# Hyena gates as seven-product pairs in the attention stage; values and token sums in the hyena stage

## The chip, the cores and the metric

The kernel runs on one core of a Trainium2 chip. The core has TensorE (PE; its weight loads are listed as PEld), VectorE (DVE), ScalarE (ACT), GpSimd (POOL) and SyncE (SP), and 16 DMA engines. DMAs are issued from the queues of SP, ACT and POOL. The metric is the time of one execution in device microseconds. The median of three runs of the kernel before is 900.05 us (899.94 to 900.84).

## The reference

One layer works on 128 context tokens and 512 latent tokens, 640 in all, with 1024 channels. After an adaLN modulation, `h = x * (1 + scale) + shift`, one projection `z = h @ w_in` gives twelve groups of 1024 columns: three for the hyena branch, its gate, queries, keys, values, the attention gate, and two merge gates.

- Hyena branch: a three-tap convolution over the three groups, `u = v_h * x1`, a long convolution of `u` with filters made by a small network (by Fourier transform), then `y_h = (conv + u * d) * x0`.
- Attention branch: 16 heads of 64. The latent tokens attend to a clamped window with a learned two-dimensional bias and to 128 cached context keys, in one softmax; the context tokens attend to themselves.
- Merge: `p_h = (y_h * silu(g_h)) @ w_bh`, `p_a = (y_a * silu(g_a)) @ w_ba`, `out = (sigmoid(m_h) * p_h + sigmoid(m_a) * p_a) @ w_out`, then `layer_norm(alpha * x + gate * out)`.

The context tokens' keys and values are outputs too.

## The kernel before, in words

Channels lie on the 128 partitions, tokens along the free dimension: a row is 128 x 640. The modulated input stays on chip as two parts, `hH` (rounded to the matmul's format) and `hL` (the rest), and so does every weight: high x high, low x high and high x low are the three passes of each product. A weight tile covers 128 output channels and all 1024 input channels; its high part is an ACT copy and its low part a difference.

There are two ways to project. `proj` does one tile: 8 blocks of input channels x 3 passes x 2 halves of 320 columns = 48 matmuls. `pair_tile` does two tiles at once by a seven-product scheme: it needs sums and differences of four weight quarters (`wsum`, 128 x 512, line 1027, in the pool `sp`), their high and low parts (`prep`, which calls `split`, lines 101 and 102), token sums `t1` to `t4` of `hH` and `hL` (`token_sums`), and 7 x 4 x 3 = 84 matmuls of 320 columns (line 1054), then a few additions of results (lines 1061 to 1069). Weight parts go round in a ring of five buffers.

The stages follow one another. The *prologue* makes the modulation. The *hyena stage* runs four quarters of two row tiles. For each, `quarter_head` projects and convolves the values and x1, and `quarter_tail` projects x0 and the gate; both use `proj` with the low part of the weights completed by an accumulating DMA on POOL's queue (`wtile` with "dma", lines 147 to 149). The long convolution (`long_conv`, `long_conv_back`) and the next filter (`filter_spectrum`) are woven into these projections by `weave`, which steps two generators in a given ratio. `gated` products of rows (`gapped_product`, lines 457 and 461) are DVE work; a finished row goes to DRAM as `yh_d`. The fourth tail is the *hand-over* (`hand_over`), which is woven with the last convolution and also does queries, keys and values 0, attention gate 0, and queries, keys and values 1. When the convolution is done, `attention_setup` closes its buffer pools and opens those of attention (`sp`, `tp`, `at`).

The *attention stage* goes through eight pairs of heads (`attend`), each woven with other projections (`mains`). In heads 0 and 1 these are three `proj` tiles each and the token sums, on DVE; from head 2 on, pairs (`queries_keys`, `gates_a`, `mix` for the merge gates), two values and one single gate. The softmax's bias comes from a mask and a table, subtracted on POOL for each head (`bias_tile`, lines 807 to 811), and POOL normalizes the probabilities (lines 840 and 891). The *merge* projects both branches, and the output with its norm comes last.

A planner decides the order on each engine from the program's order and its own estimate of times. PE's order is the program's own in the prologue and in attention; loads of the prologue keep their order, too. A buffer's tag with `bufs` slots makes the next user wait for a free slot.

## Time and profile before

| | us |
|---|---|
| median of three runs | 900.05 |
| span of the profiled execution | 898.9 |
| PE busy | 878.5 |
| DVE busy | 625.1 |
| ACT busy | 423.6 |
| POOL busy | 161.6 |

The profile is of one execution; its span runs from the first to the last instruction. Stages are read by stretches of the span: the hyena loop lies between 57 and about 285 us, the hand-over reaches to about 385, attention runs to 715, the merge and output to the end. In tables of stages, each engine has its busy time and, in brackets, its number of instructions in that stretch. In lists of groups, the part behind the first bar is busy time, the mean duration of one in ns, then the idle time of the engine just before them and what ended it. In a tile's or a line's list, durations are shortest/median/longest in ns. In an engine's order of time, the first number is the start, the second the duration, `x` the number of instructions merged in the row.

### The profile page before, as it was taken

Reading aid. Unit: us, or ns where it says so; the run is one execution under the profiler, and the core shown is the slowest. Engines: PE = TensorE matmul, PEld = TensorE weight load, DVE = VectorE, ACT = ScalarE, POOL = GpSimd, SP = SyncE. Lnnn points to the kernel's source line nnn. Section 1 sums busy time; section 2 is a strip of 40 time slices with the busy share of each in tenths; the row PEclk is TensorE's granted clock in tenths of the full one; section 3 lists DMA queues with packets and bytes.
Section 4 is the critical chain, followed back from the end, with each engine's and each line's share of the span. In section 5 each row is a group of like instructions: output and inputs, shape, how many; then the busy total and the mean of one; then the engine's idle time right before and its main releaser. Section 6 shows DMA issues by size and latency. Waiting matters only on the chain. (4 is left out here: it accounts for less than half of the span.)

```text
span 898.9 us, 16950 instructions
## 1 busy us (share of the span) xinstructions
PE 878.5 (98%) x6560; PEld 848.8 (94%) x6560; DVE 625.1 (70%) x1229; ACT 423.6 (47%) x909; POOL 161.6 (18%) x188
## 2 busy tenths in 40 slices
PE   8999999999999999999999999999999999999994
PEld 7899999999999999999999999899999999999883
DVE  4776784794778568578877578766766668667665
ACT  4495455645445342365566455555655522233100
POOL 0010010101001000086654321332332000000000
PEclk9999999999999999999999999999999999999997
DMA  9975665665647223333233332332343588355332
GB/s 335 384 170 130 136 136 118 152 129 125 157 101 153 62 69 90 93 106 92 57 126 116 104 97 90 118 117 92 102 135 106 171 298 286 133 178 172 114 103 85
DMA packets 56715, 124.43 MB, mean 138 GB/s; under 512 B 8603, under 2 KB 28059, under 8 KB 56636
## 3 DMA queue, kind: packets, MB, share of 16 engines
q1 hardware_dynamic: 46988, 103.07, 35.6%
q0 software_dynamic: 4032, 14.68, 10.1%
q10 hardware_dynamic: 5616, 5.61, 1.8%
q8 instruction: 52, 0.85, 0.4%
q14 instruction: 27, 0.22, 0.1%
HBM read 109.18 MB, written 14.16 MB: 137 GB/s over the span
## 5 line engine op out<-in xcount | busy, mean ns | idle before, releaser
L168 PE MATMUL mm<-hH,wh 128*128 128x320 f32 x672 | 160.2, 312 | 1.8 <-ACT zs L471 1.0
L168 PE MATMUL mm<-hH,wl 128*128 128x320 f32 x672 | 158.5, 310 | 0.5 <-DVE wl L102 0.4
L168 PE MATMUL mm<-hL,wh 128*128 128x320 f32 x672 | 158.6, 311 | 0.0
L168 PEld LDWEIGHTS mm<-hH,wh 128*128 128x128 f32 x672 | 112.9, 188 | 4.7 <-issue 1.8
L168 PEld LDWEIGHTS mm<-hH,wl 128*128 128x128 f32 x672 | 113.5, 188 | 1.5 <-DVE wl L102 0.9
L168 PEld LDWEIGHTS mm<-hL,wh 128*128 128x128 f32 x672 | 113.3, 188 | 1.1 <-DVE hL L315 0.5
L1054 PE MATMUL sp<-t,wb 128*128 128x320 f32 x672 | 105.4, 310 | 0.0
L1054 PEld LDWEIGHTS sp<-t,wb 128*128 128x128 f32 x672 | 99.5, 188 | 0.3 <-issue 0.3
L1054 PE MATMUL sp<-hH,wb 128*128 128x320 f32 x336 | 82.1, 313 | 0.6 <-DVE c L1069 0.5
L101 ACT ACTIVATE wh<-raw 128x1024 fp32r<-128x1024 f32 x37 | 39.1, 1060 | 71.4 <-PE mm L168 41.5
L148 POOL DMA_DIRECT2D wl<-wall x28 | 24.4, 871 | 261.8 <-ACT wl L147 224.2
L102 DVE TENSOR_TENSOR wl<-raw,wh 128x1024 fp32r<-128x1024 f32 x37 | 45.8, 1240 | 26.4 <-ACT wh L101 26.2
L1054 PEld LDWEIGHTS sp<-hH,wb 128*128 128x128 f32 x336 | 57.9, 188 | 2.8 <-issue 1.7
L149 ACT ACTIVATE wh<-raw 128x1024 fp32r<-128x1024 f32 x28 | 29.7, 1060 | 52.7 <-PE mm L168 52.6
L101 ACT ACTIVATE wb<-s 128x512 fp32r<-128x512 f32 x56 | 34.7, 626 | 40.8 <-DVE s L1027 27.7
L102 DVE TENSOR_TENSOR wb<-s,wb 128x512 fp32r<-128x512 f32 x56 | 39.0, 702 | 19.4 <-ACT wb L101 19.1
L1054 PE MATMUL sp<-hL,wb 128*128 128x320 f32 x168 | 51.8, 309 | 0.0
L840 POOL TENSOR_SCALAR p<-p,sm 128x384 f32<-128x384 f32 x32 | 45.2, 1422 | 25.7 <-DVE sm L839 25.7
L1288 PE MATMUL out<-woh,yhs 128*128 128x512 f32 (+1 forms) x176 | 45.5, 372 | 0.0
L168 PE MATMUL mm<-yhs,wh 128*128 128x320 f32 x224 | 42.6, 309 | 0.0
L840 POOL TENSOR_SCALAR edge<-edge,sm 128x320 f32<-128x320 f32 x32 | 42.1, 1326 | 2.8 <-DVE sm L839 2.8
L1288 PEld LDWEIGHTS out<-woh,yhs 128*128 128x128 f32 x176 | 32.0, 188 | 6.0
(358 smaller groups left out, 2028.9 us busy)
## 6 DMA issues: line engine op xcount, KB each, us to landing
raw<-wall SPq DMA_DIRECT2D x96, 512.0 KB, 3.7
wl<-wall POOLq DMA_DIRECT2D x28, 512.0 KB, 5.6
ada<-wada SPq DMA_DIRECT2D x16, 512.0 KB, 8.2
gate<-wgate SPq DMA_DIRECT2D x8, 512.0 KB, 4.3
wo<-wall SPq DMA_DIRECT2D x8, 512.0 KB, 4.3
xt<-xT SPq DMA_DIRECT2D x8, 320.0 KB, 7.9
dec<-decay SPq DMA_DIRECT2D x20, 128.0 KB, 3.2
yh_d<-yh SPq DMA_DIRECT2D x8, 320.0 KB, 2.5
```

What stands on the lines that cost most here:

```text
L101: hi = nc.scalar.activation(dst_h, src, AF.Copy)
L102: return hi, (eng or nc.vector).tensor_tensor(dst_l, src, f(dst_h), op=ALU.subtract)
L148: nc.gpsimd.dma_start(wl, a["wall"][i], accum_op=ALU.add)
L149: nc.scalar.activation(wh, raw[:], AF.Copy)
L168: nc.tensor.matmul(ps[hf][:, :HALF], wt[k], x[:, hf * HALF : (hf + 1) * HALF], start=(i == 0 and k == 0), stop=(i == lead[2] and k == NK - ...
L840: nc.gpsimd.tensor_scalar_mul(pv, pv, sm[:, 2:3])
L1054: nc.tensor.matmul(dst, wk, x(xi, k), start=j < 4 and k == 0 and i == 0, stop=k == 3 and i == 2, skip_group_check=True,)
L1288: ins = nc.tensor.matmul(dst, m[k][:, c0 : c0 + P], w[:, c : c + n], start=(first and k == 0), stop=(last and k == 5), skip_group_check=True,)
```

## The change

- The eight hyena gates leave the hyena stage. `quarter_tail` keeps only x0, now in the pool `yhp`. Its product with the convolution's result is made on POOL (`product_in_blocks`) and goes to DRAM as `yu_d`. In attention four pairs (`gates_h`) make the gates, POOL multiplies each half row by the reloaded product, and the result goes to `yh_d` from POOL's queue.
- All attention gates are pairs (a0, a2, a4, a6), and so are queries and keys 2 and 3. Heads have their pairs from a list, 22 in all.
- Values 1, 2 and 3 are projected in the three quarters of the hyena loop, go to DRAM (`v_d`) and are loaded again before heads 2, 4 and 6. Values 0 stay in the hand-over.
- The token sums are made on POOL during the hyena loop, a piece at every sixth step, stored to DRAM (`tok_d`) from POOL's queue and loaded in `attention_setup`.
- A pair's weights are prepared by a generator of their own (`prepared`), one product ahead at each product done, the ring of five running on from pair to pair. One of the four weight sums and three of the seven low parts are on POOL.
- The bias of each head comes ready from the host, 128 x 1024, with signs of scores turned; mask and table are gone.

```diff
+    def product_in_blocks(y, x, u):
+        nc.gpsimd.tensor_tensor(y[:, :LP], x[:, :LP], u[:, :LP], op=ALU.mult)
+        (xs, us), yb = (by_row(t[:, GAP:NG]) for t in (x, u)), y[:, SC : SC + LS]
+        for b0, n, bs in ((0, 1, slice(7, 8)), (1, 7, slice(0, 7))):
+            nc.gpsimd.tensor_tensor(from_blocks(yb[:, 64 * b0 : 64 * (b0 + n)], n), xs[:, :, bs], us[:, :, bs], op=ALU.mult)
...
     def gate_conv(n):
         if n in half_done:
-            gapped_product(out["yh"][n], out[f"u{n // 2}"][n % 2])
-            nc.sync.dma_start(yh_d[n], out["yh"][n][:])
+            y = row(yhp, "yh", f"yu{n}")
+            product_in_blocks(y, out["x0"].pop(n), out[f"u{n // 2}"][n % 2])
+            nc.gpsimd.dma_start(yu_d[n], y)
...
-            x0 = hwa.tile([P, NG + 1], F32, tag="cv", bufs=2, name=f"x0_{n}")
-            yield from conv_tile(16 + n, x0)
-            yield
-            yh[n] = row(yhp, "yh", f"yh{n}")
-            yield from gate_tile(24 + n, yh[n][:], "dma")
-            gapped_product(yh[n], x0)
+            out["x0"][n] = row(yhp, "yh", f"x0_{n}", n=NG + 1)
+            yield from conv_tile(16 + n, out["x0"][n])
             gate_conv(n)
...
     for q in range(3):
-        weave(chain(quarter_head(q + 1), quarter_tail(q)), chain(long_conv(q), braid(long_conv_back(q), filter_spectrum(q + 1))),
-              8 * NK, N_CONV + N_BACK + N_FILTER)
+        weave(along(chain(quarter_head(q + 1), quarter_tail(q), values((2, 3, 1)[q], v_d)), sums, 6),
+              chain(long_conv(q), braid(long_conv_back(q), filter_spectrum(q + 1))), 6 * NK + N_VALUES, N_CONV + N_BACK + N_FILTER)
...
-        yield from chain(queries(0), keys(0), values(0), gate_a(0), queries(1))
+        yield from chain(queries(0), keys(0), values(0), queries(1))
         out["slots_r"] = left.enter_context(tc.tile_pool(name="slots_r", bufs=1))
-        yield from chain(keys(1), values(1))
+        reload_values(1)
+        yield from keys(1)
...
+    ON_POOL = dict(sums=(3,), lows=(0, 4, 5))
...
+        for j in range(7):
+            if j == 3:
+                wsum(3, a21, a22, ALU.add)
+                wsum(6, a12, src[1], ALU.add, src[1])
+            n = len(made)
+            w = made[i0, j] = wp.tile([P, 2, 512], F32R, tag=RING[n % 5], bufs=2 if RING[n % 5] == "wh" else 3, name=f"wb{i0}_{j}")
+            split(w[:, 0], w[:, 1], src[j], nc.gpsimd if j in ON_POOL["lows"] else None)
+            yield
...
+    def gates_h(m):
+        yu = {}
+        for i, hf in ((1, 1), (0, 0), (1, 0), (0, 1)):
+            yu[i, hf] = halfrow("yu", 3, f"yur{m}{i}{hf}")
+            load_to(yu[i, hf], yu_d[2 * m + i][:, CS[hf]])
+
+        def use(i, hf, src):
+            th = halfrow("th", 2, f"th{m}{i}{hf}")
+            nc.scalar.activation(th, src, AF.Tanh, scale=0.5)
+            gate(th, src)
+            nc.gpsimd.tensor_tensor(th, th, yu[i, hf], op=ALU.mult)
+            nc.gpsimd.dma_start(yh_d[2 * m + i][:, CS[hf]], th)
...
-    weave(hand_over(), chain(long_conv(3), long_conv_back(3), attention_setup()), 6 * NK + N_VALUES, N_CONV + N_BACK + 1)
+    weave(hand_over(), chain(long_conv(3), long_conv_back(3), attention_setup()), 4 * NK + N_VALUES, N_CONV + N_BACK + 1)
...
+    HEADS = ("a0 h0", "q2 h1 m0", "q3 m1 a2", "q4 h2 m2", "q5 m3 a4", "q6 h3 m4", "q7 m5 a6", "m6 m7")
```

The new `token_sums` does the same additions as before on `nc.gpsimd`, and for each sum makes the two parts there and stores both:

```diff
+        def keep(name, t):
+            at_ = 4 * SUMS.index(name) + 2 * r
+            hi, lo = (row(yhp, "yh", f"{name}{r}{i}", F32R) for i in range(2))
+            nc.gpsimd.tensor_copy(two(hi), t)
+            nc.gpsimd.tensor_tensor(two(lo), t, f(two(hi)), op=ALU.subtract)
+            for i, x in enumerate((hi, lo)):
+                nc.gpsimd.dma_start(tok_d[at_ + i], f(x))
```

More of the change, by code (lines that the diff above doesn't have):

```diff
@@ L799, in attention_setup @@
         yield
[L801 removed]
+    at = sp = tp = None
+    tok = {t: [[], []] for t in SUMS}
     def bias_tile(hd):
[L804 to L811 removed]
+        tm = at.tile([P, 1024], F32, tag="tm", bufs=4, name=f"tm{hd}")
+        load_to(tm[:], a["bias"][hd])
         return tm
@@ L1418, in _layout @@
     rpbT = g["rpb"][0][:, ri, ci]
+    bias = np.full((16, 128, 1024), -BIG, np.float32)
+    for c in (192, 448, 704):
+        bias[:, :, c : c + 128] = 0.0
+    half, qc8 = np.arange(128) // 64, np.arange(128) % 8
+    qc = half * 8 + qc8
+    spans = (
+        (0, 24, 64, np.maximum(qc - 8, 0)), (320, 16, 0, qc), (576, 16, 128, qc - 16), (832, 24, 0, 8 + np.minimum(qc - 8, 0)),
+    )
+    for c, w, b0, lo in spans:
+        j = np.arange(8 * w)
+        key = (j // 64) * 8 + j % 8
+        ok = (key[None] >= lo[:, None]) & (key[None] < lo[:, None] + 16)
+        bias[:, :, c : c + 8 * w] = np.where(ok[None], rpbT[:, :, b0 : b0 + 8 * w], bias[:, :, c : c + 8 * w])
     ck = g["cache_k"][0, 0].reshape(128, 8, 128).transpose(1, 2, 0)
```

289 lines of the change are left out of this document (139 added, 150 removed).

## The prediction

> **What bounds the kernel now.** I read the page's first two parts first (who is busy, and when), then the table of stages, then TensorE's order of time for the price of one matmul.
>
> ```profile
> span 898.9 us, 16950 instructions
> PE 878.5 (98%) x6560; PEld 848.8 (94%) x6560; DVE 625.1 (70%) x1229; ACT 423.6 (47%) x909; POOL 161.6 (18%) x188
> PE   8999999999999999999999999999999999999994
> PEclk9999999999999999999999999999999999999997
> ```
>
> TensorE (PE) is busy 98% of the span at full granted clock; its 20 idle us lie mostly in the last slice, where the last norm runs, and in the first. A matmul removed should therefore shorten the span, as long as the others keep up. The stages (hyena, hand-over, attention, merge), with all engines:
>
> ```profile
> core 0: us, PE busy (x) PEld busy (x) DVE busy (x) ACT busy (x) POOL busy (x), PEclk, DMA share, GB/s
> 57.00:285.00 228.00, 226.69 (x1591) 224.44 (x1590) 165.71 (x260) 123.29 (x237) 21.63 (x25) 1.00 0.62 135
> 285.00:383.00 98.00, 98.00 (x732) 97.77 (x731) 63.22 (x112) 35.43 (x78) 3.03 (x17) 1.00 0.30 88
> 383.00:715.00 332.00, 329.19 (x2658) 318.02 (x2657) 238.89 (x610) 190.12 (x486) 133.12 (x129) 1.00 0.35 106
> ```
>
> VectorE (DVE) is next: 73% in the hyena loop, 65% in the hand-over, 72% in attention. GpSimd (POOL) is nearly free before attention and at 40% in it. The price of a matmul is not its duration (about 310 ns, pipelined) but the step from one start to the next:
>
> ```profile
> 173.50 0.46 PE L168 MATMUL mm<-hH,wh 128*128 128x320 f32 x2
> ...
> 174.38 0.46 PE L168 MATMUL mm<-hH,wh 128*128 128x320 f32 x2
> ...
> 500.06 0.64 PE L748 MATMUL v<-wh,hH 128*128 128x256 f32 x4
> 500.53 0.64 PE L748 MATMUL v<-wh,hL 128*128 128x256 f32 x4
> ...
> 560.89 1.93 PE L1054 MATMUL sp<-t,wb 128*128 128x320 f32 x12
> 562.66 0.38 PE L946 MATMUL ptp<-pack,pp 128*128 128x128 f32 x2
> ```
>
> A projection issues six between 173.50 and 174.38, 0.147 us each; a seven-product pair twelve between 560.89 and 562.66, also 0.147; a values matmul of 256 columns 0.47/4 = 0.12.
>
> **The change part by part.** *Matmuls.* A projected tile is 8 x 3 x 2 = 48 matmuls, 7.06 us; two are 96. A pair does two tiles in 7 x 4 x 3 = 84, 12.35 us, so each pair saves 12, 1.76 us. New pairs: four for the eight hyena gates, two for attention gates 0, 1, 2 and 7, two for queries and keys 2 and 3. Eight pairs, 96 matmuls, **14.1 us less** on the engine that sets the end. Values keep their count (120 x 0.12 = 14.4 us each) and only move. That is the floor: 898.9 - 14.1 = 884.8 of span.
>
> *Where the filler goes.* The long convolution is a chain through DVE, ScalarE (ACT) and PE; projections fill PE beside it. In each of the first three quarters two gate tiles (14.1 us) go and one values tile (14.4 us) comes: even. In the hand-over nothing comes: two gate tiles, attention gate 0 (3 x 7.06 = 21.2) and values 1 (14.4) leave, 35.6 us of filler. The rows at the border, DVE's last convolution products and PE's first scores, and prices of what comes after (count, then shortest/median/longest in ns, or busy us, mean ns and the idle time before):
>
> ```profile
> 375.28 2.23 DVE L628 SCALAR_TENSOR_TENSOR u<-u,hyd,y 128x512 f32<-128x512 f32 x2
> 377.42 0.48 DVE L457 TENSOR_TENSOR yh<-yh,u 128x128 f32<-128x128 f32 x2
> 377.82 1.42 DVE L461 TENSOR_TENSOR yh<-yh,u 128x64 f32<-128x64 f32 x4
> ...
> 389.03 0.33 PE L818 MATMUL s<-k,q 64*128 64x128 f32 x2
> ...
> 390.26 0.34 PE L818 MATMUL s<-kl,q 64*128 64x384 f32 x2
> ...
> L807 POOL TENSOR_TENSOR tm<-mask,tb x16: 591/602/1646, 383.6 to 634.9; 128x192 f32<-128x192 f32 x16
> L810 POOL TENSOR_TENSOR tm<-mask,tb x16: 732/744/1325, 384.2 to 605.3; 128x256 f32<-128x256 f32 x16
> L1027 DVE TENSOR_TENSOR s<-raw,raw 128x512 f32<-128x512 f32 x14 | 10.0, 712 | 36.7 <-DMA raw<-wall 36.7
> L102 DVE TENSOR_TENSOR wb<-s,wb x56: 675/690/1076, 439.8 to 706.9; 128x512 fp32r<-128x512 f32 x56
> L101 ACT ACTIVATE wb<-s x56: 612/628/661, 437.5 to 706.2; 128x512 fp32r<-128x512 f32 x56
> ```
>
> From 192 to 256 elements a two-input operation on GpSimd costs 0.141 us more, so undisturbed estimates are 1.30 us at 512, 0.87 at 320, 1.58 at 640, and 1.9 for one convolution product (128 + 64 + 448).
>
> The attention pools open when the convolution's pool closes, at 379.2, 9.8 us before PE needs them. With 35.6 us less filler PE is there at 353.4. The first product of a pair needs only raw weights, so PE can go on for 1.8 us and some 1.5 us of scores (the rows put them at 389.03 to 390.6), to 356.7. The second product needs a weight sum, which lies in the new pool. If the chain ended where it does now, the last two products, now on GpSimd behind a DVE step of which the first half is done at 376.4, would end at 376.4 + 2 x 1.9 = 380.2; two sums, a cast and a low part (0.71 + 0.71 + 0.63 + 0.69) take 2.7 us more, to 382.9, a wait of 26.2. What shortens the chain is the DVE's relief:
>
> ```profile
> L481 DVE SCALAR_TENSOR_TENSOR yh<-yh,mm x16: 480/482/509, 115.3 to 317.3; 128x320 f32<-128x320 f32 x16
> L461 DVE TENSOR_TENSOR yh<-yh,x x16: 218/432/647, 117.8 to 318.7; 128x64 f32<-128x64 f32 x8, 128x448 f32<-128x448 f32 x8
> L461 DVE TENSOR_TENSOR yh<-yh,u x16: 212/429/647, 156.7 to 378.6; 128x64 f32<-128x64 f32 x8, 128x448 f32<-128x448 f32 x8
> L457 DVE TENSOR_TENSOR yh<-yh,x x8: 284/286/311, 117.5 to 318.3; 128x128 f32<-128x128 f32 x8
> ```
>
> Per gate tile 2 x 0.48, and twice (0.29 + 0.86, the two blocks being twice the median of the pair): 3.3 us off DVE, 6.5 a quarter, 26 in all. If the chain were bound by DVE all through, the 26 would eat the wait; if only by latency, nothing would. I count the relief for three quarters, where DVE is 73% busy, and none in the hand-over, where it is 65%: 19.5 of 26.2, leaving **6.7 us** of wait; bounds 0 and 26.2.
>
> *Pairs in attention.* The 332 us hold 14 pairs (172.9), seven projected tiles (49.4), two values (28.8) and therefore 81 us of the heads' own work, 10.1 a head. After: 22 pairs (271.7) + 81 = 352.7. DVE gives one of four weight sums and three of seven low parts of every pair to GpSimd, and the token sums leave it. What GpSimd pays there already, the normalizations:
>
> ```profile
> L840 POOL TENSOR_SCALAR edge<-edge,sm x32: 1079/1088/2416, 396.2 to 691.1; 128x320 f32<-128x320 f32 x32
> L840 POOL TENSOR_SCALAR p<-p,sm x32: 1235/1277/2305, 400.3 to 687.9; 128x384 f32<-128x384 f32 x32
> L891 POOL TENSOR_SCALAR pp<-pp,smp 128x128 f32<-128x128 f32 x16 | 9.5, 606 | 85.6 <-DVE smp L889 57.9 <-ACT edge L838 27.7
> ```
>
> In attention: 32 x (1.079 + 1.235) + 9.7 = 83.7 of normalization as now, 88 x 1.30 = 114 of sums and low parts, 16 x 0.87 = 14 of gate products: 212 us of 353, 60%. The minima against the maxima (591 and 1646 at 192 elements) show that operations here stretch beside others; with the stretch of the normalizations (1.2) throughout, GpSimd is 72% busy. DVE drops by 22 x (0.71 + 3 x 0.69) = 61 us and gains eight pairs. No engine is full. What remains are waits; PE's idle in this stage is 332 - 329.2 = 2.8 us with 14 pairs, so 22 get 4.4: **+1.6 us**. Bounds: 0, and the second rival.
>
> The Trainium skill, "SBUF — State Buffer", section "SBUF: two separate sides", says that GpSimd and a DVE operation with two SBUF inputs share a port pair as an exclusive lock: the other blocks fully. By it GpSimd's 212 would add to the DVE's two-input work (154 sums and low parts x 0.69 and 24 gates x 0.48 = 118): 330 of 353, but in head 0 (two pairs, one of them hyena gates) 24.4 + 12.6 = 37.0 against PE's 34.8, and the sum below would be 2.2 higher. The stretched maxima agree in direction; a DVE maximum of 1.08 beside an operation of 1.1 to 1.3 is short of a full block, so I keep the rows' sum.
>
> *Token sums and products on GpSimd in the hyena stage.* The load that completes each weight's low half is issued from GpSimd's queue, and new work comes to stand before it:
>
> ```profile
> L148 POOL DMA_DIRECT2D wl<-wall x28 | 24.4, 871 | 261.8 <-ACT wl L147 224.2 <-PE ut L531 19.7 <-ACT uh L101 10.5
> ...
> L168 PEld LDWEIGHTS mm<-hH,wl 128*128 128x128 f32 x672 | 113.5, 188 | 1.5 <-DVE wl L102 0.9 <-DMA wl<-wall 0.4
> L147 ACT ACTIVATE wl<-raw 128x1024 fp32r<-128x1024 f32 x28 | 30.0, 1071 | 0.2 <-DMA raw<-wall 0.2
> wl<-wall POOLq DMA_DIRECT2D x28, 512.0 KB, 5.6
> ```
>
> The new work is 34 operations x 1.58 + 8 products x 1.9 + 24 stores x 0.87 = 90 us, on an engine that is busy 24.7 of 326. PE waited 0.4 us in all for a low half's load. The ring of three low halves lets it be issued about two tiles (14 us) ahead; less cast (1.1) and landing (5.6) some 7 us are free, and the longest piece, two operations and two stores, is 4.9. I cost it at nothing; with the cover gone it is up to 4.9 us at each of 26 loads.
>
> *The rest.* Some 26 MB more pass the queues (token tiles and gated rows out and back, values out and back, bias 512 KB a head in place of 128): on 106 GB/s in attention, nothing. On SyncE's queue all loads follow the waits for their buffers; behind a late one stand the raw weights, for which DVE waits already (36.7 us above) without PE idling. Half the 5.2 MB of token tiles has buffers outside the closing pool. The second product needs 1.3 MB of them, 4 us at the 335 GB/s of the first slice, beside the 2.7 us of sums, so within the bounds above. Sign flips and the bias ready from the host cost nothing on the path.
>
> **Sum.** 898.9 - 14.1 + 6.7 + 1.6 = 893.1 of span; the profiled execution's span lies 1.15 under the median of 900.05, so **894.3**.
>
> **The rivals.** *One: the convolution chain is bound by latency, and PE starves at the border.* For it: in the hand-over DVE is idle 35 of 98 us while the chain still takes until 379. Against it: DVE work is what lies between its steps in the loop. Full price 26.2: 900.05 - 14.1 + 26.2 + 1.6 = 913.8. It decides from 12.5 us of wait on; this is the one on the other side.
>
> *Two: GpSimd's low parts come late.* A low part behind four normalizations (2 x 1.09 + 2 x 1.28 = 4.7) with its cast and itself takes 0.63 + 4.7 + 1.3 = 6.6 us; the ring of five lets it start four products (7.1 us) ahead. With the two prompt normalizations as well (1.2) it is 0.7 late, and with the contended 1.6 of a 512 operation 1.0; at two bursts a head that is 16 us, 910. Against it: products are further apart wherever a head's own work stands between them, and the planner may put the low part first. It decides from 0.33 us a pair.
>
> *Three: the filler and the chain meet exactly and nothing is lost*: 900.05 - 14.1 = 886. For it the full DVE relief of 26. *Four: gains and waits cancel*, 898.3 to 901.9, any sum of waits between 12.3 and 16.
>
> **How the numbers follow.** Forecast with its neighbours, 887 to 898, 0.46; the third 0.18; the first 0.18; the second 0.10; the fourth 0.08. A difference under 0.2% (1.8 us) can't be told from none here. Faster 0.64, same 0.08, slower 0.28. The likeliest case's own range is 887 to 898; signs are mixed, so the range goes from the floor, 885, to near the first rival's full price, 911.
>
> **What would show it.** The changed profile should have 96 fewer matmuls of 320 columns, attention about 353 us from its first scores, which should stand near 360, with PE idle some 7 us around them; DVE under 65% in attention, GpSimd near 70%. The forecast is wrong if PE idles over 12 us at the border (waiting for weight sums or token tiles), if weight loads in attention wait on GpSimd's low parts, or if the hyena stage itself grows because low halves land late.

## The result, and the profile after

The changed kernel takes 968.1 us (median of four runs, 966.6 to 971.1) against 900.0 of the kernel before (899.6 to 900.8). The ratio is 1.0747, 95% interval 1.0719 to 1.0774: 68 us slower, where 6 us faster was forecast. The profiled execution has a span of 964.8 us.

First the page's lines for TensorE and GpSimd, and TensorE's granted clock, in 40 slices of 24 us:

```profile
span 964.8 us, 17002 instructions
...
PE 892.5 (93%) x6464; PEld 850.8 (88%) x6464; DVE 666.8 (69%) x1179; ACT 441.2 (46%) x950; POOL 346.2 (36%) x330
...
PE   8799999799999997798988989999898999999994
...
POOL 0740115542210304584764666556746500000000
PEclk9999999899999998899999999999999999999997
```

TensorE has the 96 matmuls less (6464 for 6560) and is nevertheless busy 14 us longer. It has pauses now in the second slice, in the eighth (at 185 us, in the hyena stage), at the border to attention (the 16th and 17th) and all through attention, and the clock row dips at the longest of them. GpSimd, nearly free before attention in the old kernel, works in both stages.

Then busy time by stage. The borders are the first filter matmul, the start of attention (first scores before the change, first pair's matmul after it), and the last pair's matmul. First the kernel before:

```profile
core 0: us, PE busy (x) PEld busy (x) DVE busy (x) ACT busy (x) POOL busy (x), PEclk, DMA share, GB/s
0.00:54.90 54.90, 52.03 (x526) 45.45 (x527) 33.53 (x65) 28.96 (x53) 2.02 (x14) 1.00 0.88 320
54.90:389.00 334.10, 332.79 (x2382) 330.05 (x2381) 232.25 (x376) 163.79 (x319) 30.91 (x51) 1.00 0.52 121
389.00:715.20 326.20, 323.39 (x2610) 312.39 (x2610) 237.86 (x609) 187.35 (x484) 127.73 (x123) 1.00 0.36 107
715.20:898.00 182.80, 170.29 (x1047) 160.86 (x1045) 121.44 (x181) 43.51 (x57) 0.93 (x2) 0.97 0.51 173
```

And the changed kernel:

```profile
0.00:62.10 62.10, 54.28 (x526) 47.24 (x527) 42.27 (x64) 29.27 (x54) 25.07 (x32) 0.97 0.81 297
62.10:366.70 304.60, 294.75 (x2145) 291.95 (x2145) 224.31 (x291) 149.05 (x291) 77.49 (x84) 0.99 0.58 141
366.70:777.00 410.30, 371.14 (x2752) 349.23 (x2751) 278.26 (x644) 218.53 (x550) 242.71 (x212) 0.96 0.42 136
777.00:964.00 187.00, 172.33 (x1047) 162.35 (x1045) 121.95 (x181) 44.33 (x57) 0.93 (x2) 0.97 0.49 170
```

In attention TensorE idles 39 us (410.3 less 371.1) for 2.8 before, and the granted clock averages 0.96. To separate work from loss, I gave each matmul the median start-to-start distance of its line and shape in the trace before (0.147 us for 320 columns) and took the sum off each stage, the merge ending with the last matmul. What is left over is idle time, slow clock and stretched spacing. The same sums for all runs of this study, each with its own matmuls, in us, with the time of each run. From e1 on each time is one execution, but for j1 and j2 (the median of ten). The kernel before took 899.8 to 903.4 us beside the single ones, and 897.8 to 903.6 in 19 executions on one chip, so a difference of up to 4 us between two of them is not read as an effect.

| kernel | time | start | hyena | attention | merge |
|---|---|---|---|---|---|
| matmul work before / after | 858.7 / 844.5 in all | 44.2 / 44.2 | 331.8 / 291.3 | 312.9 / 339.2 | 169.8 / 169.8 |
| left over: before | 900.0 | 10.7 | 2.4 | 13.2 | 0.4 |
| after | 968.1 | 17.9 | 13.3 | 71.0 | 4.3 |
| e1 pairs off GpSimd | 945.7 | 18.3 | 13.1 | 50.2 | 2.2 |
| e3 token sums not early | 972.5 | 10.8 | 24.5 | 72.7 | 4.2 |
| e4 token sums on VectorE | 960.2 | 10.8 | 10.5 | 75.4 | 2.9 |
| f1 = e1 and e4 | 935.5 | 11.4 | 10.3 | 52.3 | 1.5 |
| f2 = f1, third raw buffer, no product | 927.6 | 11.1 | 40.1 | 13.1 | 1.3 |
| f3 = f1, no product | 935.4 | 11.0 | 10.3 | 51.7 | 2.1 |
| f4 = f1, five token tiles early | 934.9 | 10.7 | 10.3 | 50.7 | 2.8 |
| g1 = after, third raw buffer | 949.9 | 18.3 | 13.0 | 54.0 | 2.2 |
| g2 = f1, third raw buffer | 927.0 | 11.6 | 10.3 | 40.6 | 2.2 |
| g3 = g2, five token tiles early | 915.3 | 11.0 | 10.3 | 32.2 | 1.6 |
| g4 = g3, one key tile later | 930.4 | 11.5 | 38.9 | 16.7 | 3.0 |
| h1 = g4, its weights earlier | 918.9 | 11.6 | 18.6 | 23.3 | 2.5 |
| h2 token sums in attention | 912.2 | 10.8 | 8.4 | 26.8 | 0.7 |
| i1 = before, pairs on GpSimd | 917.5 | 11.2 | 2.2 | 30.8 | 1.3 |
| i2 = before, Hyena gates moved | 935.7 | 10.8 | 33.0 | 24.7 | 1.6 |
| j1 = before, ready bias | 900.3 | 10.8 | 2.0 | 14.3 | 0.4 |
| j2 = j1, third raw buffer | 905.7 | 11.8 | 3.2 | 16.0 | 1.3 |

The floor fell by 14.2 us, as forecast. The left-over rose by 7.2 + 10.9 + 57.8 + 3.9 = 79.8, and 79.8 - 14.2 = 65.6 is the difference of the spans (65.9). So the question is what fills 58 us in attention and 18 before it. The 4 us of the merge aren't followed up.

The waits of the changed kernel (engine, what waited, for whom: us in all, times, longest):

```profile
DVE s L1049 <- DMA raw<-wall: 42.4, 18, 5.0
...
ACT wb L101 <- DMA raw<-wall: 24.6, 12, 3.7
PEld sp L1080 <- POOL wb L102: 13.6, 8, 6.0
PE pt L915 <- ACT ptsp L1009: 13.1, 7, 3.5
...
PE sp L1080 <- POOL wb L102: 11.4, 7, 5.7
```

Three suspects show at once: GpSimd's low parts, for which TensorE itself waits; the raw weights, for which VectorE and ScalarE wait; and a late ScalarE copy (`ptsp`), which stands behind the pairs' high parts in ScalarE's order.

### The profile page after: what moved, and what is told of

It reads as the page before. It is cut to its first block, busy times and chain, and to the rows that moved or that the text cites. A ratio compares the mean times of both kernels' runs of the same rounds, so it can differ in the third digit from the quotient of the medians.

```text
span 964.8 us, 17002 instructions
## 1 busy us (share of the span) xinstructions
PE 892.5 (93%) x6464; PEld 850.8 (88%) x6464; DVE 666.8 (69%) x1179; ACT 441.2 (46%) x950; POOL 346.2 (36%) x330
## 5 line engine op out<-in xcount | busy, mean ns | idle before, releaser
L1080 PE MATMUL sp<-t,wb 128*128 128x320 f32 x1056 | 180.4, 323 | 22.6 <-POOL wb L102 11.4
L1080 PEld LDWEIGHTS sp<-t,wb 128*128 128x128 f32 x1056 | 164.6, 196 | 30.0 <-POOL wb L102 13.3
L1080 PE MATMUL sp<-hH,wb 128*128 128x320 f32 x528 | 128.1, 314 | 0.0
L102 POOL TENSOR_TENSOR wb<-raw,wb 128x512 fp32r<-128x512 f32 x66 | 89.5, 1360 | 87.9 <-ACT wb L101 79.6
L170 PE MATMUL mm<-hH,wh 128*128 128x320 f32 x416 | 100.5, 315 | 4.2 <-ACT hH L316 4.0
L170 PE MATMUL mm<-hH,wl 128*128 128x320 f32 x416 | 99.9, 312 | 0.4 <-DVE wl L102 0.4
L170 PE MATMUL mm<-hL,wh 128*128 128x320 f32 x416 | 99.7, 312 | 0.3 <-DVE hL L317 0.3
L102 DVE TENSOR_TENSOR wb<-s,wb 128x512 fp32r<-128x512 f32 x88 | 71.1, 819 | 14.4 <-ACT wb L101 14.1
L170 PEld LDWEIGHTS mm<-hL,wh 128*128 128x128 f32 x416 | 71.1, 190 | 1.5 <-DVE hL L317 1.1
L170 PEld LDWEIGHTS mm<-hH,wl 128*128 128x128 f32 x416 | 71.1, 190 | 1.5 <-DVE wl L102 0.9
L101 ACT ACTIVATE wb<-raw 128x512 fp32r<-128x512 f32 x66 | 41.1, 623 | 34.7 <-DMA raw<-wall 24.6
L1080 PEld LDWEIGHTS sp<-hL,wb 128*128 128x128 f32 x264 | 50.0, 189 | 0.0
L1049 DVE TENSOR_TENSOR s<-raw,raw 128x512 f32<-128x512 f32 x22 | 16.8, 762 | 43.3 <-DMA raw<-wall 42.4
L101 ACT ACTIVATE wh<-raw 128x1024 fp32r<-128x1024 f32 x21 | 22.1, 1059 | 52.3 <-PE mm L170 41.5
```

Source lines behind the costliest of these rows:

```text
L101: hi = nc.scalar.activation(dst_h, src, AF.Copy)
L102: return hi, (eng or nc.vector).tensor_tensor(dst_l, src, f(dst_h), op=ALU.subtract)
L170: nc.tensor.matmul(ps[hf][:, :HALF], wt[k], x[:, hf * HALF : (hf + 1) * HALF], start=(i == 0 and k == 0), stop=(i == lead[2] and k == NK - ...
L1049: (nc.gpsimd if j in ON_POOL["sums"] else nc.vector).tensor_tensor(src[j], x, y, op=op)
L1080: nc.tensor.matmul(dst, wk, x(xi, k), start=j < 4 and k == 0 and i == 0, stop=k == 3 and i == 2, skip_group_check=True,)
```

## The experiments

Each kernel is the changed one with the edit shown, unless it says otherwise.

### GpSimd's share of the pairs

```diff
-    ON_POOL = dict(sums=(3,), lows=(0, 4, 5))
+    ON_POOL = dict(sums=(), lows=())
```

> The changed kernel (968 us) with all four weight sums and all seven low parts of a pair on DVE, nothing of them on GpSimd. Theory A (GpSimd's two-input operations come late and slow DVE down beside them): the attention stage, 404 us from first scores to the merge, shrinks by 25 us or more, total 930 to 945; DVE's 512-element low parts go back from 819 ns to about 700. Theory B (with 22 pairs in a row the two raw weight buffers turn round too slowly, whoever makes the low parts): little change, 955 to 968, and DVE's and ACT's waits for raw weights stay at 40 us or more.

Measured 945.7 us, 22.4 less than the changed kernel; nearly the whole gain is in attention (left over 71.0 to 50.2). That is nearer to the first theory, and short of its 25; the waits for raw weights fell as well, from 42.4 and 24.6 us to 23.7 and 27.1 (VectorE, ScalarE), so this run alone doesn't separate the two. The opposite edit, into the kernel before:

```diff
-            nc.vector.tensor_tensor(src[j], x, y, op=op)
+            (nc.gpsimd if j == 3 else nc.vector).tensor_tensor(src[j], x, y, op=op)
...
-            split(wb[j][:, 0], wb[j][:, 1], src[j])
+            split(wb[j][:, 0], wb[j][:, 1], src[j], nc.gpsimd if j in (0, 4, 5) else None)
```

> The kernel before with one edit: in its 14 pairs, the fourth sum and the low parts of the first, fifth and sixth product on GpSimd, as the change has them; the pairs' five-ahead ring stays inside each pair. Taking this off the changed kernel's 22 pairs gave 22.4 us, 1.0 us a pair. If GpSimd's 1.3 to 1.7 us operations (0.7 on VectorE) delay the pairs by themselves, 14 pairs cost 10 to 18 us here: 910 to 918 us. If they only hurt with pairs back to back and too few raw buffers, the ordinary tiles between the pairs hide them: 898 to 904 us.

Measured 917.5 us beside 903.4 on the same chip, 14.1 us for 14 pairs, 1.0 us each (against the profile before, from another execution, the span is 16.8 us longer, 1.2 each). This is the cleanest finding of the study: the offloading costs time by itself, in a kernel that has nothing else of the change. Its attention stage, and TensorE's longest waits in it:

```profile
389.40:733.10 343.70, 328.88 (x2611) 314.29 (x2611) 225.72 (x553) 187.92 (x484) 206.47 (x178) 0.99 0.34 101
...
PE sp L1054 <- ACT wb L101: 4.4, 3, 2.9
...
PE sp L1054 <- POOL wb L102: 3.5, 3, 1.7
...
PE sp L1054 <- DVE wb L102: 3.4, 6, 2.2
```

VectorE has 12 us less to do than before the change (225.7 for 237.9), and TensorE idles 14.8 us for 2.8. Its waits end with GpSimd's low parts, but as much with ScalarE's high parts and VectorE's low parts; the list of the kernel before has none of the three. How the two engines meet is seen in the list of the raw tiles' users in the changed kernel between 450 and 720 us (durations in ns, shortest/median/longest):

```profile
L102 POOL TENSOR_TENSOR wb<-raw,wb x46: 1258/1292/1832, 451.2 to 711.4; 128x512 fp32r<-128x512 f32 x46
...
L1049 DVE TENSOR_TENSOR s<-raw,raw x16: 691/693/1667, 452.1 to 713.4; 128x512 f32<-128x512 f32 x16
...
L1049 DVE TENSOR_TENSOR s<-raw,s x16: 669/684/1784, 457.3 to 717.4; 128x512 f32<-128x512 f32 x16
```

and the same list with the pairs off GpSimd:

```profile
L1049 DVE TENSOR_TENSOR s<-raw,s x17: 680/685/695, 452.9 to 717.4; 128x512 f32<-128x512 f32 x17
...
L1049 DVE TENSOR_TENSOR s<-raw,raw x16: 681/692/694, 468.6 to 713.3; 128x512 f32<-128x512 f32 x16
```

A low part takes 1.29 us on GpSimd where VectorE needs about 0.69. And VectorE's own sums, 0.69 us alone, reach 1.78 beside GpSimd: longer by 1.1 us, nearly a whole GpSimd operation. I counted it over the 154 sums and low parts that VectorE makes in the changed kernel's attention: 23 start during a two-input operation of GpSimd, and 22 of these last over 0.75 us, with a median of 1.40; 15 start during a normalization (one tensor and a column of factors), and 13 of these stay under 0.75, the longest being 0.96. Which of the two makes more of the 1.0 to 1.2 us a pair, the slow operation or the blocked neighbour, these runs don't separate.

The Trainium skill, "SBUF — State Buffer", section "SBUF: two separate sides", says that a GpSimd operation and a VectorE operation with two SBUF inputs exclude each other for a whole instruction. The prediction weighed this rule and dropped it, since the longest VectorE row before was 1.08 us; the 1.67 and 1.78 us here agree with it beside two-input operations of GpSimd, and the rows beside normalizations mostly don't show it.

### Token sums on GpSimd

The planner had moved the token sums up into the prologue. The start's two halves, before:

```profile
27.00:54.90 27.90, 27.73 (x284) 25.27 (x283) 18.95 (x36) 17.09 (x34) 1.04 (x1) 1.00 0.83 294
```

and after:

```profile
27.00:54.90 27.90, 22.78 (x237) 19.96 (x236) 23.86 (x31) 10.58 (x19) 17.61 (x12) 0.94 0.71 274
```

GpSimd works 17.6 of 27.9 us there, VectorE does five instructions fewer in five more microseconds, and TensorE does 47 matmuls fewer. The first edit holds the sums at their place in the program, in the hyena loop:

```diff
-        nc.gpsimd.tensor_tensor(a_, part(hH, 0, 1), part(hL, 0, 1), op=ALU.add)
+        tc.keep_in_program_order(nc.gpsimd.tensor_tensor(a_, part(hH, 0, 1), part(hL, 0, 1), op=ALU.add))
```

> The changed kernel with the first operation of the token sums kept behind what the program issued before it on GpSimd, so that the sums can't move up into the prologue (they start there at 26 us). If their operations beside DVE's cost the prologue its 7 us (first filter matmul at 62.1 where it was at 54.9): that stands again at 55 and the total falls by 5 to 9 us, to about 960. If the prologue is late for another reason: no change.

Measured 972.5 us, not the 960 expected. The start is mended (left over 10.8, as before the change), and the hyena stage pays for it (24.5). The second edit holds them there and makes them on VectorE:

```diff
...
-        nc.gpsimd.tensor_copy(two(hi), t)
-        nc.gpsimd.tensor_tensor(two(lo), t, f(two(hi)), op=ALU.subtract)
+        nc.vector.tensor_copy(two(hi), t)
+        nc.vector.tensor_tensor(two(lo), t, f(two(hi)), op=ALU.subtract)
...
```

> As the run before, and the token sums' additions and parts made on DVE instead of GpSimd (their stores stay on GpSimd's queue). If what hurts the hyena stage is DVE and GpSimd getting in each other's way (DVE 12 us over its undisturbed time between 160 and 200): 5 us or more faster than the run before, in spite of some 31 us more work on DVE, since GpSimd's 60 us vanish. If DVE's load is what counts there: slower than the run before by 5 to 20 us.

Measured 960.2 us, 12.3 below the run before. The hyena stage's first part with the sums held on GpSimd:

```profile
54.00:115.00 61.00, 52.48 (x342) 50.36 (x341) 51.48 (x52) 29.88 (x61) 28.02 (x25) 0.92 0.63 150
```

and on VectorE:

```profile
54.00:115.00 61.00, 60.88 (x430) 60.07 (x429) 48.73 (x76) 37.05 (x76) 10.33 (x14) 1.00 0.74 182
```

VectorE does 76 instructions in 48.7 us, 24 more than the 52 in 51.5 us that it does beside GpSimd: taking work over made it less busy. The same four rows show it, first beside GpSimd's sums, then without them:

```profile
L102 DVE TENSOR_TENSOR dftL<-draw,dftH x4: 1332/2955/4556, 56.4 to 64.3; 128x640 fp32r<-128x640 f32 x4
...
L102 DVE TENSOR_TENSOR dftL<-draw,dftH x4: 812/818/819, 54.1 to 56.4; 128x640 fp32r<-128x640 f32 x4
```

TensorE goes from 342 to 430 matmuls in the same 61 us. Against the changed kernel, in which the planner had spread the sums over both stages, the gain is 7.9 us. This edit and the one of the pairs together:

> GpSimd out of the two-input work of both stages: the pair sums and low parts are VectorE's in attention, and the token sums are VectorE's in the hyena stage, kept in the order in which they are written. Alone the first gave 945.7 us and the second 960.2 us against 968.1. If the two losses are separate, one in attention and one before it, they add: 937.8 us, hyena stage about 302 us, attention about 390 us. If the slower VectorE work of the hyena stage only pushed the border wait along, the border wait (6.9 us for a token tile) takes back the second gain and the run is at 944 to 946 us.

Measured 935.5 us: the gains add, as far as single executions show it (22.4 + 7.9 from 968.1 makes 937.8).

### Raw weight buffers

A pair's raw weights lie in a pool of two buffers. A third one in all stages (run e2) has no room: the hyena stage's pool takes 24.1 KB a partition and 20.75 were left, so there is no time for it. In the kernel with GpSimd out of both, ScalarE and VectorE still wait long for raw weights in attention, and TensorE for ScalarE's copy `ptsp`, as long as in the changed kernel:

```profile
ACT wb L101 <- DMA raw<-wall: 30.0, 12, 5.5
...
DVE s L1049 <- DMA raw<-wall: 25.5, 19, 3.7
...
PE pt L915 <- ACT ptsp L1009: 13.1, 6, 3.3
```

A third buffer in attention's pool `at` (`late[0]`, once that pool is open) takes every third raw tile but the merge's:

```diff
-        raws[i] = wp.tile([P, 1024], F32, tag="raw", name=f"raw{i}")
+        n_raw[0] += 1
+        pool, tag, bufs = (late[0], "rawA", 1) if late and i < T_BH and n_raw[0] % 3 == 0 else (wp, "raw", 2)
+        raws[i] = pool.tile([P, 1024], F32, tag=tag, bufs=bufs, name=f"raw{i}")
```

Its 4 KB a partition were found first by leaving out the gates' product with `yu` and its reload; a run without them and with two buffers is its reference.

> As the kernel with both, with the product of the Hyena gates with the convolution output and its reload left out, two raw buffers: the reference for the run with three. 16 products on GpSimd and 16 loads of 160 KB go. If they are hidden, the time is within 3 us of the kernel with both (about 938 us); if the gates' hand to GpSimd holds the pairs up (ScalarE's tanh waits 5.8 us for the store), it is 5 us or more below.

> As the kernel with both, and a third raw buffer in attention beside the two, its room made by leaving out the product of the Hyena gates with the convolution output and that product's reload (the gates go to DRAM without it). Theory of the raw buffers: the turn of buffer free, load of 3.4 to 6 us, sum, split holds up the pairs, so VectorE's and ScalarE's waits for raw (20 and 22 us in attention without GpSimd) shrink to under 10 us and attention is 10 to 20 us shorter than in the kernel without the product and with two buffers. Theory of the engine that splits: the waits only move to the rings behind, attention within 4 us of that kernel.

Measured 935.4 and 927.6 us: the product is hidden with two buffers, and the third one gains 7.8 us. Attention with two buffers:

```profile
356.70:747.80 391.10, 364.61 (x2754) 349.24 (x2753) 288.39 (x731) 217.84 (x550) 108.88 (x109) 0.97 0.41 136
```

and with three:

```profile
384.80:739.10 354.30, 352.99 (x2756) 342.02 (x2756) 285.94 (x722) 216.30 (x542) 102.40 (x97) 1.00 0.39 126
```

354.3 us, 1.3 idle, full clock. 22 pairs can be fed; VectorE is 81% busy and no bound. But 28 of the 36.8 us are only moved, for the start of attention came 28 us later, since the third buffer's first tile, in memory that the convolution still holds, was a weight of an ordinary tile ahead of the border: TensorE waited 22.0 us for it. The next three kernels let only pairs use the buffer, keep the product, and find the room in a bias buffer less:

```diff
-        tm = at.tile([P, 1024], F32, tag="tm", bufs=4, name=f"tm{hd}")
+        tm = at.tile([P, 1024], F32, tag="tm", bufs=3, name=f"tm{hd}")
```

> The changed kernel as it is, GpSimd work and all, with a third raw buffer for the pairs in attention; its room comes from one bias buffer less (three, the second bias of a head fetched two blocks later). If the raw buffers are the main cause in attention, the buffer that GpSimd's slow low parts hold (1.3 us each) no longer starts the next load late: attention falls from 410.3 us by 30 us or more, to 930 to 940 us in all. If the third buffer only helps where GpSimd is out of the way, it gains under 12 us here (956 us or more).

> GpSimd out of both stages (935.5 us with two raw buffers) and the third raw buffer, nothing left out of the computation, the buffer used by pairs only and from attention's first head on. Attention without border waits was 354.3 us in the run that left a product out, against 391.1; here the border waits for token tiles (10 us, and some 8 us of slow clock behind them) stand in attention again, so 354 + 10 to 18 = 364 to 372, and 908 to 916 us in all. If the missing product was a part of that gain, it is 925 us or more.

Measured 949.9 us (18.2 gained, less than the 30 of the first case, more than the 12 of the second) and 927.0 us (8.5 gained from 935.5; 908 to 916 was expected). In the second the wait of the sums for raw weights is down from 25.5, that of ScalarE's high parts is gone from the list, and with it most of TensorE's for `ptsp`, which stands behind them on ScalarE:

```profile
DVE s L1055 <- DMA raw<-wall: 15.8, 16, 3.1
...
PE pt L919 <- ACT ptsp L1015: 3.0, 1, 3.0
```

So the third suspect is in the main the second, as TensorE sees it. The buffer helps, with GpSimd at work too, so both causes overlap: 21 us (pairs off GpSimd) and 17 us (third buffer) of attention's 58, one by one; 30 together (71.0 to 40.6; 35 from the 75.4 of e4, which has the token sums on VectorE as this kernel has). Much of the rest stood at the border.

### The border

At the first pair TensorE goes through these rows in the changed kernel (start, duration, what; in square brackets the idle time before and what ended it):

```profile
379.88 2.41 PE L1080 MATMUL sp<-t,wb 128*128 128x320 f32 x6 [0.26 <-DMA t<-tok_d]
387.97 0.60 PE L1080 MATMUL sp<-t,wb 128*128 128x320 f32 x1 [5.67 <-POOL wb L102]
389.44 6.74 PE L1080 MATMUL sp<-t,wb 128*128 128x320 f32 x28 [0.87 <-DMA t<-tok_d]
```

and the stretch as a whole:

```profile
377.80:394.60 16.80, 9.89 (x32) 8.45 (x33) 7.18 (x17) 5.79 (x17) 8.95 (x13) 0.50 1.02 393
```

32 matmuls in 16.8 us, at half clock, while the transfers run at 393 GB/s with all 16 engines busy. At 0.147 us each they are 4.7 us of work, so 12.1 us are lost here. With GpSimd out of the way the token tiles alone are the wait there (5.0 us in one piece, 3.5 in another). Reading five of the 16 token tiles back before the last convolution ends:

```diff
...
+        for name, i in (("t2", 0), ("t2", 1), ("t3", 0), ("t3", 1), ("t1", 0)):
+            t = row(yhp, "yh", f"{name}_0{i}", F32R)
+            tok[name][i].append(t)
+            load_to(f(t), tok_d[4 * SUMS.index(name) + i])
         hwa_stack.close()
```

> As the kernel with both, with five of the 16 token tiles read back before the convolution of the last quarter ends, so that four fewer loads of 320 KB stand ahead of the second and third product of the first pair. If the token tiles' way through DRAM makes the border wait (1.1 and 6.9 us by the gaps of TensorE, and the 17 us at half clock behind them), the border shortens by 4 to 6 us of idle time and up to 8 us of slow clock: 925 to 934 us. If the border is bound by the memory traffic as a whole (276 GB/s there), the same wait moves to the next product and the run is within 3 us of the kernel with both.

> The same with five of the 16 token tiles read back early, which gained 0.6 us where the pairs waited for raw buffers. If that wait had hidden the gain, the early tiles are now worth 3 to 6 us (905 to 911 us); if the border is bound by the memory traffic as a whole, under 1.5 us.

With two raw buffers it gave nothing that can be read (934.9, 0.6 less), with three 11.7 us (915.3, against 927.0; 8.4 of it in attention), more than the 3 to 6 expected: the raw wait had hidden it. Then an ordinary tile as cover at the border:

```diff
-        yield from keys(1)
+        yield
...
         items = HEADS[j].split()
+        if j == 0:
+            yield from keys(1)
```

> The same, and the keys of head pair 1, an ordinary tile of 48 matmuls (7.1 us), moved from the hyena stage's end to the start of attention, ahead of the first pair, as cover for the token tiles. If the token tiles come at a fixed time, the 6 to 10 us of border waits shrink by up to 7 us and TensorE keeps its clock: 894 to 903 us. If the convolution chain then lacks that cover at its end, the same wait shows before the first scores and the run is within 2 us of the one without the move.

Measured 930.4 us, neither of the two cases. TensorE waited 20.6 us for this tile's weights: their load was issued at 371.1 us, behind nine token loads of which the first, at 359.8, waited for the convolution's memory. By the program's count this is the 36th raw tile and, asked for in attention now, falls to the third buffer, so its own place lay in that memory too, as in f2. Attention behind that wait took 357.5 us, product and all, like the 354.3 above: once the border is paid, the stage runs. With these weights loaded ahead (into one of the two old buffers):

> As the run with the keys of head pair 1 at the start of attention, and their weights fetched before the token tiles are queued. In that run TensorE stood 20.6 us for these weights, whose load stood behind 11 token loads that wait for the hyena stage's memory. If that queue was the whole loss there, the 20.6 us go and the border costs less than in the run without the move (913.5 us of span, of which 9 us idle at the border): 900 to 908 us. If the cover is missing at the end of the convolution chain, the gaps of 1.3 and 2.1 us before it stay and the run is at 912 us or more.

Measured 918.9 us. The 20.6 us go, but gaps of 2.4 and 1.8 us appear in the convolution's back transform and one of 4.5 us before later scores (for VectorE), so the move doesn't pay: the second case. Since the edit changed the queue place and the buffer at once, it doesn't say which of the two made the 20.6 us. Hyena stage and attention together leave 41.9 us over, 42.5 without the move.

### Which part pays alone

The token tiles' way through DRAM undone: the sums back on VectorE in heads 0 and 1 of attention, with the ordinary tiles there, and 19 pairs from head 2 on:

```diff
-    HEADS = ("a0 h0", "q2 h1 m0", "q3 m1 a2", "q4 h2 m2", "q5 m3 a4", "q6 h3 m4", "q7 m5 a6", "m6 m7")
+    HEADS = ("", "", "q4 m0 a2", "h0 m1 m2", "q5 q6 a4", "h1 h2 m3 h3", "q7 m4 a6", "m5 m6 m7")
...
+        if j < 2:
+            yield from alongside(chain(*([gate_a(1)] if j == 0 else []), queries(j + 2), keys(j + 2)), token_sums(j), 8)
```

> The token tiles' way through DRAM undone: token sums on VectorE in heads 0 and 1 of attention as before the change, with the ordinary tiles (gates 0 and 1, queries and keys 2 and 3) that stood there, and 19 pairs from head 2 on in place of 22 from head 0; GpSimd out of the pairs, three raw buffers, the product's reload two at a time. TensorE's work is 3 x 12 x 0.147 = 5.3 us more than with 22 pairs, 8.8 us less than before the change. If the border and the pairs' preparation are all that the change lost beyond the hyena stage's 8 us, this ends at 886 to 898 us, below the kernel before. If 19 pairs in six heads are too many for VectorE and ScalarE (three pairs a head against 14 in six), waits in heads 2 to 7 return and it is 900 to 915 us.

Measured 912.2 us: 12.3 over the kernel before on its chip, where g3 was 13.9 over it, so the two are even, and no kernel with the moved gates is better. Its stage of pairs alone, 431 to 726 us, has 5.5 us idle in 295 with VectorE at 82%; the larger losses lie in front, in 360 to 400 us, where it is idle 6.6 us and the clock is 0.83. Only the Hyena gates moved, and nothing else of the change but the ready bias:

> Only the Hyena gates moved: pairs in heads 2, 3, 5 and 6 of attention (18 pairs), their product on GpSimd through DRAM as changed; the values, the gates of attention, later queries and keys and the token sums stand as before the change, all pair work on VectorE, two raw buffers, ring inside each pair. TensorE's work: 4 x 12 x 0.147 = 7.1 us less than before. If the attention of before has room for four more pairs, the hyena stage must run 56 us shorter with the gate tiles gone: 893 to 897 us. If the hyena stage's convolution chain doesn't shrink with them (the changed kernel put 35 us of values there), TensorE waits in each quarter and the run is at 903 to 930 us, with the gaps in the stage before attention.

Measured 935.7 us, beyond both cases. The hyena stage and attention:

```profile
55.00:363.30 308.30, 287.72 (x1998) 280.35 (x1997) 211.84 (x312) 143.70 (x287) 41.48 (x55) 0.98 0.45 111
363.30:750.30 387.00, 375.11 (x2946) 363.34 (x2946) 281.23 (x688) 210.59 (x530) 125.16 (x113) 1.00 0.40 123
```

Matmul work in the hyena stage fell by 56.5 us (331.8 to 275.3), its time by 25.8 (334.1 to 308.3): the convolution's chain doesn't shrink with the projections beside it. That is why the change had to put the values there. Attention with 18 pairs leaves 24.7 us over, for 13.2 with 14. Last, two parts in the kernel before, without any moved tile: the bias ready from DRAM, and with it the third raw buffer.

> The kernel before with the change's bias tiles alone: the 16 bias tiles of 512 KB come ready from DRAM in place of 128 KB and a mask that GpSimd combines (three operations a head), and the scores keep their sign. GpSimd's 48 operations go, 6 MB more are loaded. VectorE has 86% busy time in heads 0 and 1 and is slowed there by GpSimd; without it 1 to 3 us: 897 to 899 us. If those heads are covered by TensorE's work anyway, or the loads collide with the weights, 899 to 902 us.

> The same with the third raw buffer in attention (three bias buffers). It gained 8 to 18 us where 22 pairs stand back to back. With 14 pairs and ordinary tiles between them TensorE waits 2.7 us in attention in all, so 1 to 3 us more: 895 to 898 us, below both kernels. If what attention loses beyond its matmuls (13 us) is not the raw buffers, it is within 1 us of the run without it.

Measured 900.3 us, ratio 0.9993 (0.9973 to 1.0013), and 905.7 us, ratio 1.0036 (1.0025 to 1.0046). The bias makes no difference; the kernel with the buffer that gained 8 to 18 us with 22 pairs is 0.4% over the one before with 14, though VectorE's wait for raw weights falls from 34.9 us to 21.1. Why it loses isn't shown: the edit also takes a bias buffer away and lets ordinary tiles use the third buffer, and 1.0 us of the loss lies in the start, which the buffer can't reach. No kernel of this study is faster than the one before.

## Why the prediction was wrong

- *Matmuls, -14.1 us.* Right: 14.2 by the sums above.
- *Pairs in attention, +1.6.* This step failed most: it stretched the idle time of 14 pairs (2.8 us) to 22 in proportion. Measured, 57.8 more is left over in the stage, 12.1 of it at the border and some 46 among the pairs. The old pairs stood between ordinary tiles that need little of VectorE; 22 pairs back to back show what the tiles had covered. By the runs: GpSimd's sums and low parts 21 (alone), two raw buffers 17 (alone), 30 together; early token tiles then 8 more. Against the left-over of before (13.2), 19 of the 58 stay in the best kernel with 22 pairs (g3); that most of it lies at the border is concluded from the 354.3 and 357.5 us stages behind a paid border, not shown by a run of its own. The forecast of 352.7 us for the stage is nearly reached by those two: it needs the third buffer, VectorE alone, and the token tiles there.
- *Raw weights "for which DVE waits already ... without PE idling".* The wait was slack with 14 pairs (a third buffer shortens it and gains nothing) and none with 22.
- *The second rival, low parts late on GpSimd, 910 us.* The right operations, with a chance of 0.10; they were priced at 16 us, and the runs give 14 to 17 (in the kernel before, with 14 pairs) and 21 to 22. That the price nearly fits is partly luck: the mechanism named, a low part queued behind normalizations, ends only 3.5 us of TensorE's waits in the kernel before with this part alone, and VectorE's blocking, which the rival left out, is beside it. It alone would not have made 968.
- *Token sums at nothing.* Failed. The step looked only at GpSimd's own queue, the low halves' loads. The cost lay on VectorE, which runs slower beside GpSimd: 7.2 us in the prologue, where the planner had put the first of them, which the step didn't foresee, and some 3 in the hyena stage (13.3 against 10.5); all held in the hyena stage they cost 14.0 there (24.5 against 10.5).
- *The lock rule, rejected at 2.2 us.* The maximum of 1.08 us before came from a stage in which GpSimd did little two-input work. With such work in it the maximum is 1.78, and 22 of 23 rows that start beside it are stretched.
- *Filler in the hyena stage, "even".* Also failed: with the token sums on VectorE the stage still leaves 8 us more than before (10.3 for 2.4).
- *The border, +6.7 from the convolution chain.* The place was right, the cause not, and the size was 12.1. First scores were named near 360 and come at 374.5; with the sums on VectorE at 364.6, so the chain, for which DVE's relief was counted against 26.2, ended soon enough. The wait comes behind the first scores, for token tiles and, in the changed kernel, a low part of GpSimd. The tiles' 5.2 MB were costed at 1.3 MB and 4 us; but all 16, two bias tiles and the raw weights go through one queue at once.
- *What it would show.* GpSimd near 70% and VectorE under 65% in attention: 59% and 68% (242.7 and 278.3 of 410.3). Neither engine was full; the loss was in the order of the waits, as the text said, and not in the sum that it made.
- *The clock.* No term for it. Many a pause brought 3.4 us or more at half speed; the mean granted clock fell from 0.994 to 0.972 of the span.

What stays open: the cause of the 8 us in the hyena stage, in which two gaps of 2.4 and 2.8 us end with a ScalarE copy out of PSUM; the 4 us of the merge; and what of GpSimd's cost is blocking and what is its own slowness.

## What to carry to other kernels

Idle time on the bound engine doesn't scale with the count of dense units: before packing them together, look at what the loose units between them cover (here the loads of raw weights with two buffers), and at the waits that are now slack on other engines. Price work given to GpSimd on VectorE too: put the offloaded operations alone into the old kernel and look at the longest rows of VectorE, not the median. A detour through DRAM is paid where it is read back, in the queue in which the weights stand.

## What the hardware showed

TensorE's granted clock has two values in these traces, 1.0 and 0.5, and stays at 0.5 for 3.41 us or a multiple of it (6.83 from 183.1, 17.07 from 377.7), but for the stretch that runs into the end. In the changed kernel (order of time, then stretches, the clock being the number before the DMA share):

```profile
444.86 1.38 PE L1080 MATMUL sp<-t,wb 128*128 128x320 f32 x7 [2.54 <-DVE wb L102]
...
793.25 0.57 PE L170 MATMUL mm<-yhs,woh 128*128 128x320 f32 x2 [1.85 <-DVE mh L482]
...
570.61 0.55 PE L915 MATMUL pt<-pack,p 128*128 128x128 f32 x3 [2.77 <-ACT ptsp L1009]
```

```profile
446.00:449.20 3.20, 3.20 (x14) 3.20 (x13) 2.50 (x5) 0.63 (x1) 0.00 (x0) 0.50 0.33 90
...
574.00:578.00 4.00, 4.00 (x29) 4.00 (x28) 1.06 (x2) 1.79 (x4) 2.57 (x3) 1.00 0.97 284
794.20:797.50 3.30, 3.30 (x14) 3.30 (x13) 3.29 (x5) 0.99 (x2) 0.00 (x0) 0.50 0.99 394
```

A pause of 2.54 us at 444.9 and one of 1.85 at 793.2 are followed by a slow stretch: 14 matmuls in 3.2 us, where 29 go in the 4.0 us from 574 at full clock. One of 2.77 at 570.6 is not. So a pause of 2 to 3 us can cost up to 1.7 us beside its own length (half of 3.4), and whether it does isn't decided by its length alone.

What decides it can be read off the same trace. The slow stretches of the changed kernel begin at 49.98, 183.10, 377.66, 445.92, 517.60, 643.89, 725.82, 794.08 and 954.51 us, and the distances between these are whole multiples of 3.4133 us (39, 57, 20, 21, 37, 24, 20 and 47). So the clock is set in windows on a fixed grid. The three pauses in their windows:

```profile
442.51:445.92 3.41, 1.06 (x7) 1.07 (x8) 3.41 (x3) 1.65 (x4) 3.37 (x3) 1.00 0.00 0
565.39:568.81 3.42, 2.45 (x20) 2.20 (x18) 1.67 (x6) 1.51 (x4) 3.42 (x4) 1.00 0.76 265
568.81:572.22 3.41, 1.61 (x12) 1.61 (x13) 1.39 (x2) 3.27 (x8) 3.41 (x4) 1.00 0.08 29
790.67:794.08 3.41, 1.56 (x10) 1.29 (x10) 1.57 (x4) 0.69 (x1) 0.00 (x0) 1.00 1.00 376
```

The pauses of 2.54 and 1.85 us lie inside one window each (the first but for 0.2 us), which is idle for 69 and 54%, and the next window is slow. The pause of 2.77 us is split between two, idle for 28 and 53%, and neither is followed by a slow one. I counted the windows at full clock in the 15 profiles whose grid can be found: all 78 that were idle for over 55% were followed by a slow one, 21 of 196 between 18 and 55%, and none of 3615 below.

The Trainium skill, "TensorE: Matmul & The Clock Gate", section "Part 1: The HAM clock gate", gives the same two states and a free-running window of about 3.4 us, and lets the clock drop after a whole idle window. The two states, the window of 3.4 us and its own fixed grid agree with the trace; the drop came here after pauses of half to three quarters of that window.
